# A two-layer Hymba trunk on one core: the forget gates' chain moved forward, low parts moved to GpSimd, and two plain feed-forward blocks per layer in place of three

## Chip, cores and metric

The kernel runs on one core of a Trainium2 chip. The metric is the device time of one execution in microseconds (us). Of the kernel before there are three runs: median 1271.29 us, 1268.26 to 1271.49.

Engines: PE is TensorE (matrix products; PEld is its weight load), DVE is VectorE, ACT is ScalarE, POOL is GpSimd, and SP issues DMAs.

## What is computed

512 tokens of width 1024, with 16 learned meta tokens ahead (528 columns), go through two layers:

```
xn   = rmsnorm(h);  proj = xn @ w_in            # fox q, k, v, forget logits; retention q, k, v, gate
logf = log_sigmoid(flog + b_fgate);  c = cumsum(logf)
fox: softmax(q_t.k_s / 8 + c[t] - c[s], s <= t) @ v          # 8 heads of 64
ret: sum_{s<=t} gamma^(t-s) (q_t.k_s) v_s, head norm, * silu(gate)   # 4 heads of 128
h    = h + concat(fox, ret) @ w_out
hn   = rmsnorm(h)
h    = h + (silu(hn @ w_gate) * (hn @ w_up)) @ w_down        # 2816 wide: 22 blocks of 128
```

After the second layer h is normalised once more and the meta tokens are dropped. Everything is float32, and has to stay close to float32 in precision.

## The kernel before

**Products.** Activations lie transposed, channels on partitions and tokens along the row, so h is eight tiles `h0` to `h7` of 128x528. A float32 product is made of three in the format fp32r: every operand is split into a high part (a cast) and a low part (the rest), and high x high, high x low and low x high are summed in PSUM. For weights, `convert` (L177) does this tile by tile: a 128x1024 tile `raw` comes by DMA, ScalarE casts it to `whi` (L199), and VectorE or GpSimd subtracts to make `wlo` (L202). The argument `pool` of `dense_steps` (L207) chooses: VectorE takes two subtractions of 128x512, GpSimd eight of 128x128. Activations are split into `xh` (ScalarE, L327) and `xl` (VectorE, L328).

**Norms.** A product does not wait for its norm. TensorE multiplies the raw h with its gain; the scale R of each token (`col_rstd`, L290 to L309) comes later and is multiplied in when a result leaves PSUM. `squares` (L336) makes the sum of squares `ss`, L298 adds over partitions on TensorE, L303 to L308 make R from it.

**Order.** TensorE runs in the order in which the program lists its steps: lists of small functions, into which `merge`, `spread` and `ret_places` put the steps of attention and retention at given places. The other engines' orders are chosen by a scheduler from dependencies and priorities; `tc.high_priority()` moves instructions ahead, `pin` keeps them in the program's order. PSUM has two pools: `psd` with two buffers, and `psa` with four. A product can begin only when an accumulator of its pool has been read out.

**Head of layer 0.** `start` (L1270 on) fills the time until the first data with nine matmuls on the memset tile `wide` (L1277), loads h and the first weights, and then q and k of the first pair of heads are multiplied (L225). `forget_gates` (L375) makes the eight forget logits z; `forget_sums` (L399) multiplies them by R (L403), takes log-sigmoid (Abs, Exp, Ln on ScalarE, L404 to L406; `min` and subtraction on VectorE, L407 and L408), sums along the tokens with a scan (L409) and splits the sums into `fs` (L411, L412). `q_done` (L439) reads q out of PSUM into `tq` (L442) and splits it into `qo` and `qs`; `k_done` (L453) does so for k into `kc` and `kx`, and puts the sums of the head into rows of `kc` (L467, its "own" rows). The scores (L519) multiply kc and kx with qo and qs, so the sums c[t] - c[s] come out of the same product. `ropes` (L1254) makes the rotation tables `cr` and `sr`, scaled by R.

**Feed-forward stage.** The first three of 22 blocks are plain: gate and up as full products over eight tiles of x (L225). In layer 0 these are 96 matmuls of 264 columns per block, in layer 1, which needs only the 512 real tokens, 48 of 512. `g_done` (L840, L843) reads the gate, `u_done` (L851, L852) the up part. The other 19 blocks are `Unit`s: gate and up together as a two by two block product with seven products in place of eight, 84 matmuls of half the columns each (L907). A Unit needs combined activations, the tiles `th` and `tl`, which `x_forms` (L860 on) makes from h through the tile `S` (L868 to L872, split at L151), and combined weights (L941, L942, L948, L954, split at L895 and L896). `x_forms` has four parts, put every nine steps into the plain blocks. The last tiles ahead of this stage are those of w_out's second round, whose result is added to h (L810); `scale_split` then makes xh and xl of the stage.

**Tail.** The last layer ends with the final norm, whose squares are added by VectorE (L1138) and then over the partitions on TensorE (`sums`).

Of the kernel before, what the change touches and what calls it, by code (L numbers as in the profile page):

```python
# [10 lines left out]
F32 = mybir.dt.float32  # L11
# [10 lines left out]
FH = 8  # L22
# [5 lines left out]
PLAIN = 3  # L28
# [11 lines left out]
def hybrid_kernel(ctx, tc, x_t, w_in, w_fl, w_out, w_gate, w_up, w_down, vecs, b_fg, rope, decay, mask, ident, out_t):  # L40
# [14 lines left out]
    nc.vector.memset(msk[:, 0:T - 128], 0.0)  # L55
# [11 lines left out]
    nc.vector.memset(onec, 1.0)  # L67

# [330 lines left out]
    def forget_sums(l, st):  # L399
# [7 lines left out]
        nc.vector.tensor_scalar(z, z, bfg[:, l:l + 1], 0.0, ALU.add, ALU.min)  # L407
        nc.vector.tensor_sub(z, z2, z)  # L408
# [24 lines left out]
    def fox_dense(l, g, ly, real, st):  # L433
# [20 lines left out]
        def k_done(ps):  # L454
# [3 lines left out]
            for s in range(2):  # L458
# [8 lines left out]
                (nc.gpsimd if g else nc.vector).tensor_scalar(kc[b0:b0 + 32 + FH, :], f_tiles[0].bitcast(F32), pick[:, hd:hd + 1], 0.0, ALU.mult, ALU.add)  # L467
# [345 lines left out]
    def out_proj(l, rnd, mix, real):  # L813
# [4 lines left out]
                                rnd == 0 or m2 < 2, rnd == 1 and m2 == 1) for m2 in range(NK // 2)], [])  # L818

    def ffn(l, st, real, last):  # L820
# [235 lines left out]
        for r, (f0, f1) in enumerate(ROUNDS):  # L1056
            for f in range(f0, f1):
                if f < PLAIN:
                    steps += dense_steps(w_gate[l, f], [(0, xs, NK, QC, g_done(f) if f else held.append)], banks=f == 1)
                    steps += dense_steps(w_up[l, f], [(0, xs, NK, QC, u_done(f))])  # L1060
                    continue
# [28 lines left out]
        else:  # L1090
# [34 lines left out]
            def square_b(m):  # L1125
                if m == 0:
                    t = fft("S", F32, (128, 6, w), 2)
                    fin["one"] = [t[:, i, 0:nb] for i in range(3)]
                    fin["acc"], fin["rb"], fin["tb"] = (t[:, i, 0:nb] for i in range(3, 6))
                    d = fin["acc"]  # L1130
                elif m < NK - 3:
                    fin["sq", m] = d = tt("sq")[:, 0:nb]
                else:
                    d = fin["one"][m - NK + 3]
# [101 lines left out]
        for i in range(HB):  # L1236
            steps.insert(NK + 4 + 9 * i, x_forms(i))
# [8 lines left out]
    def layer(l):  # L1246
# [68 lines left out]
        if l == 0:  # L1315
            plan += [lambda: squares(ly, FULL, True, False)] + qk[:-2] + [first_parts] + gates + qk[-2:] + stats + [lambda: ly["wait"].pop(0)()] + sums + [lambda: ly["wait"].pop(0)()]
# [9 lines left out]
        for g in range(2):  # L1326
            main, rest = fs[g]
            m0, r0, places = (((7 if l else 10.5, 31 if l else 32.5), (34, 40.5), (13, 33.5, 35.5, 37.5, 39, 40.5, 43, 44, 47.5, 48)),
# [12 lines left out]
                      ret_places(2, 26, 23.5, 24.5, 32, 28, 33.5, 36, 56.5, 40.5, 57.5),  # L1341
# [82 lines left out]
```

## Time and profile before

| | |
|---|---|
| median of three runs | 1271.29 us |
| lowest, highest run | 1268.26, 1271.49 us |
| profiled execution | 1268.53 us |
| its span, first to last instruction | 1266.7 us |
| TensorE busy | 1251.2 us, 99% |
| VectorE busy | 991.9 us, 78% |
| ScalarE busy | 704.8 us, 56% |
| GpSimd busy | 273.3 us, 22% |
| DMA | 116.19 MB, 92 GB/s mean |

A row of the timeline gives the start and the duration in us, the engine, the line, the operation, out<-in by the program's names with their shape, how many instructions the row groups, and in brackets how long the engine sat idle ahead of it and what ended that. Durations of neighbours on an engine overlap a little (matmuls more than others), so the time that an instruction takes away from its engine is the distance of two starts. A row of windows gives, for a stretch, the busy time of each engine with its instructions, the granted clock of TensorE as a share of full speed, the DMA share and GB/s. Numbers behind a name (`kc_105`) tell instances of a tile apart.

### The profile page before, as it was taken

To read this page: it belongs to the slowest core of one execution; us is meant where nothing else is said; L and a number is where in the kernel's file an instruction comes from. 1 tells how busy PE (TensorE), PEld (TensorE's weight loads), DVE (VectorE), ACT (ScalarE), POOL (GpSimd) and SP (SyncE) were. 2 spreads that over 40 slices of the span, in tenths; PEclk is the share of its full clock that TensorE was granted. 3 is DMA by queue.
4 is the path that set the end of the run, shared out by engine and by line. 5 is a ranking of instruction groups with operands and counts; after the bars stand their busy time and mean duration, and the time that the engine had idled before them with its cause. 6 is when DMAs were issued, how large, how long until landed. Compare 5 with 4: busy or idle time off the path is not lost.

```text
span 1266.7 us, 23526 instructions
## 1 busy us (share of the span) xinstructions
PE 1251.2 (99%) x9225; PEld 1194.1 (94%) x9225; DVE 991.9 (78%) x1804; ACT 704.8 (56%) x1301; POOL 273.3 (22%) x539
## 2 busy tenths in 40 slices
PE   9999999999999999999999999999999999999997
PEld 8899999999999999999999989998789999999996
DVE  8887756779988888887786877567899888888867
ACT  6766655676444444444466766557764444444445
POOL 3455546420000000000126556554100000000000
PEclk9999999999999999999999999999999999999999
DMA  6122222223333333332322122222223333333321
GB/s 218 50 76 75 76 77 72 72 67 118 104 97 100 100 101 100 101 101 84 101 77 84 60 86 74 70 90 67 100 94 123 100 101 101 100 101 101 100 84 67
DMA packets 43342, 116.19 MB, mean 92 GB/s; under 512 B 5088, under 2 KB 12000, under 8 KB 43232
## 3 DMA queue, kind: packets, MB, share of 16 engines
q1 hardware_dynamic: 42800, 114.41, 28.1%
q8 instruction: 72, 1.18, 0.4%
q14 instruction: 38, 0.31, 0.1%
q10 hardware_dynamic: 432, 0.29, 0.1%
HBM read 112.58 MB, written 2.10 MB: 91 GB/s over the span
## 4 chain that ended last, share of the span: by engine, by line
PE 93%; ACT 3%; DVE 3%; issue 1%; DMA 0%; ACTq 0%; DVEq 0%
PE psd L225 30%; PE psa L907 18%; PE psd L1042 14%; PE psd L907 13%; PE psa L225 5%; PE psa L1042 4%; PE psa L429 2%; PE psa L519 2%; PE psa L589 1%; PE psa L756 1%; PE psa L722 1%; ACT whi L199 1%; PE psa L298 0%; ACT xh L327 0%; DMA raw<-w_in 0%
## 5 line engine op out<-in xcount | busy, mean ns | idle before, releaser
L202 POOL TENSOR_TENSOR wlo<-raw,whi 128x128 fp32r<-128x128 f32 x504 | 258.2, 548 | 260.1 <-ACT whi L199 259.7
L225 PE MATMUL psd<-xh,whi 128*128 128x264 f32 (+1 forms) x792 | 195.5, 314 | 0.2 <-DVE tq L442 0.2
L225 PE MATMUL psd<-xl,whi 128*128 128x264 f32 (+1 forms) x792 | 186.7, 303 | 0.6 <-DVE xl L328 0.6
L225 PE MATMUL psd<-xh,wlo 128*128 128x264 f32 (+1 forms) x792 | 187.0, 304 | 0.0
L225 PEld LDWEIGHTS psd<-xh,whi 128*128 128x128 f32 x792 | 128.6, 189 | 5.0 <-issue 0.6
L225 PEld LDWEIGHTS psd<-xh,wlo 128*128 128x128 f32 x792 | 127.2, 188 | 6.2 <-DVE wlo L202 0.4
L225 PEld LDWEIGHTS psd<-xl,whi 128*128 128x128 f32 x792 | 127.8, 189 | 5.4 <-DVE xl L328 1.4
L199 ACT CAST whi<-raw 128x512 fp32r<-128x512 f32 (+1 forms) x168 | 97.9, 613 | 41.5 <-PE psd L225 28.4
L895 ACT CAST whi<-raw 128x1024 fp32r<-128x1024 f32 (+2 forms) x62 | 54.9, 885 | 51.3 <-PE psd L907 39.8
L895 ACT CAST fwhi<-raw 128x1024 fp32r<-128x1024 f32 (+2 forms) x62 | 55.6, 897 | 47.5 <-PE psd L907 40.0
L122 POOL MEMSET kc<- 64x528 f32 x2 | 1.1, 533 | 345.4 <-PE psa L907 345.4
L896 DVE TENSOR_TENSOR wlo<-raw,whi 128x1024 fp32r<-128x1024 f32 (+2 forms) x62 | 62.9, 1014 | 12.7 <-ACT whi L895 12.6
L896 DVE TENSOR_TENSOR fwlo<-raw,fwhi 128x1024 fp32r<-128x1024 f32 (+2 forms) x62 | 64.0, 1032 | 11.1 <-ACT fwhi L895 10.9
L907 PE MATMUL psa<-th,whi 128*128 128x264 f32 (+1 forms) x232 | 65.4, 282 | 0.0
L907 PE MATMUL psa<-th,wlo 128*128 128x264 f32 (+1 forms) x232 | 65.4, 282 | 0.0
L907 PE MATMUL psa<-tl,whi 128*128 128x264 f32 (+1 forms) x232 | 65.3, 282 | 0.0
L907 PE MATMUL psa<-th,fwhi 128*128 128x264 f32 (+1 forms) x224 | 63.4, 283 | 0.0
L907 PE MATMUL psa<-tl,fwhi 128*128 128x264 f32 (+1 forms) x224 | 63.3, 283 | 0.0
L907 PE MATMUL psa<-th,fwlo 128*128 128x264 f32 (+1 forms) x224 | 63.2, 282 | 0.0
L536 ACT ACTIVATE pr<-pr,nmax 128x144 f32<-128x144 f32 (+1 forms) x64 | 36.8, 576 | 45.4 <-DVE nmax L523 26.1
L895 ACT CAST fwhi<-S 128x1024 fp32r<-128x1024 f32 x20 | 21.0, 1049 | 68.6 <-PE psa L907 66.5
L973 ACT COPY e<-psa 128x264 f32<-128x264 f32 (+1 forms) x114 | 42.8, 376 | 28.4 <-PE psa L907 24.1
(365 smaller groups left out, 4041.2 us busy)
## 6 DMA issues: line engine op xcount, KB each, us to landing
raw<-w_in SPq DMA_DIRECT2D x54, 512.0 KB, 3.5
raw<-w_gate SPq DMA_DIRECT2D x44, 512.0 KB, 3.9
fraw<-w_up SPq DMA_DIRECT2D x38, 512.0 KB, 3.5
raw<-w_down SPq DMA_DIRECT2D x64, 256.0 KB, 2.9
raw<-w_out SPq DMA_DIRECT2D x16, 512.0 KB, 3.4
raw<-w_down SPq DMA_DIRECT2D x32, 192.0 KB, 2.5
raw<-w_up SPq DMA_DIRECT2D x6, 512.0 KB, 3.5
h<-x_t SPq DMA_DIRECT2D x8, 264.0 KB, 4.5
```

What stands on the lines that cost most here:

```text
L199: pin(nc.scalar.copy(hi, job["raw"][:, c0:c1]), pinned)
L202: pin(sub(lo[:, c:c + step], job["raw"][:, c0 + c:c0 + c + step], hi[:, c:c + step].bitcast(F32)), pinned)
L225: nc.tensor.matmul(ps[1][b][:, 0:c1 - c0], w[:, wk, :], x[:, c0:c1], start=(k == 0 and i == 0), stop=(k == n - 1 and i == 2))
L429: nc.tensor.transpose(ps[:, 128 * j:128 * j + 128], src[:, o:o + 128], idt)
L519: nc.tensor.matmul(sc[0:nq, 0:c1 - c0], qq[:, q0:q0 + nq], kk[:, c0:c1], start=(i == 0), stop=(i == 1))
L536: nc.scalar.activation(pr, pr, AF.Exp, bias=nmax[0:nq], scale=-1.0, accum_out=rsum)
L589: nc.tensor.matmul(po[:, c0:SEQ], v[:, j, :], pp[:, j, META + c0:T], start=(j == 0 and i == 0), stop=(j == 4))
L895: nc.scalar.copy(hi, src)
L896: nc.vector.tensor_sub(lo, src, hi.bitcast(F32))
L907: nc.tensor.matmul(bank()[:, 0:b.shape[-1]], a[:, o + k, :], b, start=(fresh and k == 0 and i == 0), stop=(k == n - 1 and i == 2), skip_gr ...
L973: nc.scalar.copy(self.t["e"][:, i], self.t["x"][:, 0:w])
L1042: nc.tensor.matmul(v[:, 0:c1 - c0], a[:, s * n + k, :], b[:, c0:c1], start=(k == 0 and i == 0), stop=(k == n - 1 and i == 2))
```

## The change

It has five parts.

1. `PLAIN` goes from 3 to 2: the third block of each layer becomes a Unit, and `x_forms` is put every seven steps.
2. The low parts of the plain blocks' weights, four tiles per layer, and of the last two tiles of w_out's second round go from VectorE to GpSimd.
3. In layer 0, `forget_sums` stands ahead of `q_done` and `k_done` and is given priority as a whole; the subtraction ahead of the scan is taken into the scan (add, then subtract). Of the two copies of the sums into `kc`, one is made by VectorE with priority and one by ScalarE.
4. The memset of `msk` goes from VectorE to GpSimd, and some places of steps are shifted.
5. In the tail, one more pair of squares is added on VectorE, and TensorE's sum has three operands in place of four.

```diff
-PLAIN = 3
+PLAIN = 2
...
-    nc.vector.memset(msk[:, 0:T - 128], 0.0)
...
+    nc.gpsimd.memset(msk[:, 0:T - 128], 0.0)
...
-        nc.vector.tensor_scalar(z, z, bfg[:, l:l + 1], 0.0, ALU.add, ALU.min)
-        nc.vector.tensor_sub(z, z2, z)
-        nc.vector.tensor_tensor_scan(z2, z, z, 0.0, ALU.add, ALU.max)
-        with ExitStack() if l else tc.high_priority():
+            nc.vector.tensor_scalar(z, z, bfg[:, l:l + 1], 0.0, ALU.add, ALU.min)
+            nc.vector.tensor_tensor_scan(z2, z2, z, 0.0, ALU.add, ALU.subtract)
             nc.scalar.copy(f_tiles[0][0:FH], z2)
...
-                (nc.gpsimd if g else nc.vector).tensor_scalar(kc[b0:b0 + 32 + FH, :], f_tiles[0].bitcast(F32), pick[:, hd:hd + 1], 0.0, ALU.mult, ALU.add)
+                own, of = kc[b0:b0 + 32 + FH, :], f_tiles[0].bitcast(F32)
+                if g:
+                    nc.gpsimd.tensor_scalar(own, of, pick[:, hd:hd + 1], 0.0, ALU.mult, ALU.add)
+                elif s:
+                    nc.scalar.activation(own, of, AF.Copy, scale=pick[:, hd:hd + 1])
+                else:
+                    with tc.high_priority():
+                        nc.vector.tensor_scalar(own, of, pick[:, hd:hd + 1], 0.0, ALU.mult, ALU.add)
...
-                                rnd == 0 or m2 < 2, rnd == 1 and m2 == 1) for m2 in range(NK // 2)], [])
+                                True, rnd == 1 and m2 == 1) for m2 in range(NK // 2)], [])
...
-                    steps += dense_steps(w_gate[l, f], [(0, xs, NK, QC, g_done(f) if f else held.append)], banks=f == 1)
-                    steps += dense_steps(w_up[l, f], [(0, xs, NK, QC, u_done(f))])
+                    steps += dense_steps(w_gate[l, f], [(0, xs, NK, QC, g_done(f) if f else held.append)], True, banks=f == 1)
+                    steps += dense_steps(w_up[l, f], [(0, xs, NK, QC, u_done(f))], True)
...
+                sum_b(5)
                 v = psum_a()[:, 0:nb]
-                sums(v, [fin["one"][0], fin["acc"]] + fin["one"][1:])
+                sums(v, [fin["one"][0], fin["acc"], fin["one"][1]])
...
-            steps.insert(NK + 4 + 9 * i, x_forms(i))
+            steps.insert(NK + 4 + 7 * i, x_forms(i))
...
-            plan += [lambda: squares(ly, FULL, True, False)] + qk[:-2] + [first_parts] + gates + qk[-2:] + stats + [lambda: ly["wait"].pop(0)()] + sums + [lambda: ly["wait"].pop(0)()]
+            plan += [lambda: squares(ly, FULL, True, False)] + qk[:-2] + [first_parts] + gates + qk[-2:] + stats + sums + [lambda: ly["wait"].pop(0)()] * 2
```

**VectorE at the head of layer 0.** From R (L308) on, this is its order before:

```order
L308 SCALAR_TENSOR_TENSOR R<-nwt,R 128x528
L442 SCALAR_TENSOR_TENSOR tq<-psd,R 128x528
L403 SCALAR_TENSOR_TENSOR z<-z,R 8x528
L1258 SCALAR_TENSOR_TENSOR cr<-cr,R 128x528
L450 TENSOR_TENSOR qs_427<-tq,qo_103 64x528
L456 SCALAR_TENSOR_TENSOR tq<-psd,R 128x528
L450 TENSOR_TENSOR qs_431<-tq,qo_104 64x528
L407 TENSOR_SCALAR z<-z,bfg 8x528
L473 SCALAR_TENSOR_TENSOR pd_115<-psa,R 128x264 x2
L408 TENSOR_TENSOR z<-z_435,z 8x528
L465 TENSOR_TENSOR kx_447<-tq,kc_105 64x528
L409 SCALAR_TENSOR_TENSOR z_435<-z 8x528
```

In the changed kernel the same place reads (the lines are those of the changed file: L440 is q's tq, L454 k's, L408 the scan, L478 the pd of values, L410 the low part of fs):

```order
L308 SCALAR_TENSOR_TENSOR R<-nwt,R 128x528
L403 SCALAR_TENSOR_TENSOR z<-z,R 8x528
L1264 SCALAR_TENSOR_TENSOR cr<-cr,R 128x528
L440 SCALAR_TENSOR_TENSOR tq<-psd,R 128x528
L407 TENSOR_SCALAR z<-z,bfg 8x528
L454 SCALAR_TENSOR_TENSOR tq<-psd,R 128x528
L448 TENSOR_TENSOR qs_436<-tq,qo_103 64x528
L408 SCALAR_TENSOR_TENSOR z_425<-z_425,z 8x528
L478 SCALAR_TENSOR_TENSOR pd_115<-psa,R 128x264
L448 TENSOR_TENSOR qs_440<-tq,qo_104 64x528
L478 SCALAR_TENSOR_TENSOR pd_115<-psa,R 128x264
L410 TENSOR_TENSOR fs<-z_425,fs 8x528
```

Z and cr now stand ahead of q's tq, and the scan ahead of the second half of q. What follows up to the two copies into kc was, before,

```order
L465 TENSOR_TENSOR kx_452<-tq,kc_106 64x528
L1258 SCALAR_TENSOR_TENSOR sr<-sr,R 128x528
L412 TENSOR_TENSOR fs<-z_435,fs 8x528
L644 SCALAR_TENSOR_TENSOR pd_116<-psd,R 128x528
L467 TENSOR_SCALAR kc_105<-fs,pick 40x528
L467 TENSOR_SCALAR kc_106<-fs,pick 40x528
```

and is now

```order
L463 TENSOR_TENSOR kx_446<-tq,kc_105 64x528
L472 TENSOR_SCALAR kc_105<-fs,pick 40x528
L463 TENSOR_TENSOR kx_451<-tq,kc_106 64x528
L1264 SCALAR_TENSOR_TENSOR sr<-sr,R 128x528
L649 SCALAR_TENSOR_TENSOR pd_116<-psd,R 128x528
```

The first copy (L472) moved ahead of the second kx, sr and the pd of the retention's values; the second copy left VectorE.

**VectorE at the head of the feed-forward stage, layer 0.** From the last xl to the reading of the first gate block sg, before (the S tiles are those of `x_forms`; wlo are low parts of plain blocks; L869 to L872 make S, L151 splits):

```order
L869 TENSOR_TENSOR S_4359<-S_4359 128x264
L871 SCALAR_TENSOR_TENSOR S_4359<-h5_78,vec_85,S_4359 128x264 x2
L872 SCALAR_TENSOR_TENSOR S_4359<-h5_78,vec_85,S_4359 128x264
L151 TENSOR_TENSOR tl0_4283<-S_4286,th0_4282 128x1056
L305 TENSOR_TENSOR nwt_4271<-R_4270 128x528
L151 TENSOR_TENSOR tl0_4283<-S_4359,th0_4282 128x1056
L307 SCALAR_TENSOR_TENSOR nwt_4271<-psa_4264,nwt_4271 128x264
L307 SCALAR_TENSOR_TENSOR nwt_4271<-psa_4265,nwt_4271 128x264
L202 TENSOR_TENSOR wlo_4344<-raw_4341,whi_4343 128x512
L308 SCALAR_TENSOR_TENSOR R_4270<-nwt_4271,R_4270 128x528
L202 TENSOR_TENSOR wlo_4344<-raw_4341,whi_4343 128x512
L843 SCALAR_TENSOR_TENSOR sg_4279<-psd_4149,R_4270 128x528
```

and in the changed kernel (L874 to L877 make S there, L848 reads sg):

```order
L151 TENSOR_TENSOR tl0_4309<-S_4379,th0_4308 128x1056
L877 SCALAR_TENSOR_TENSOR S_4432<-h6_79,vec_84,S_4432 128x264
L305 TENSOR_TENSOR nwt_4297<-R_4296 128x528
L874 TENSOR_TENSOR S_4485<-S_4485 128x264
L307 SCALAR_TENSOR_TENSOR nwt_4297<-psa_4290,nwt_4297 128x264
L307 SCALAR_TENSOR_TENSOR nwt_4297<-psa_4291,nwt_4297 128x264
L151 TENSOR_TENSOR tl1_4311<-S_4432,th1_4310 128x1056
L308 SCALAR_TENSOR_TENSOR R_4296<-nwt_4297,R_4296 128x528
L876 SCALAR_TENSOR_TENSOR S_4485<-h7_80,vec_84,S_4485 128x264
L848 SCALAR_TENSOR_TENSOR sg_4305<-psd_4166,R_4296 128x528
```

The low parts are gone from here, and the forms of the third and the fourth pair of tiles (S_4432, S_4485, and tl1) stand ahead of sg, which they did not before. In full the stretch has, before, six L202, eight operations on S and two tl; now one sum of squares, twelve operations on S and three tl (two in layer 1).

**GpSimd at the end of layer 0's attention.** Before, its last low part is that of the second tile of w_out's second round, and memsets for layer 1 follow:

```order
L202 TENSOR_TENSOR wlo_3600<-raw_3597,whi_3599 128x128 x8
L202 TENSOR_TENSOR wlo_3758<-raw_3755,whi_3757 128x128 x8
L202 TENSOR_TENSOR wlo_3879<-raw_3876,whi_3878 128x128 x8
L122 MEMSET kc0_8390 64x528
L91 MEMSET qo0_8388 64x528
```

In the changed kernel six more tiles follow:

```order
L202 TENSOR_TENSOR wlo_3878<-raw_3875,whi_3877 128x128 x8
L202 TENSOR_TENSOR wlo_3931<-raw_3928,whi_3930 128x128 x8
L202 TENSOR_TENSOR wlo_4014<-raw_4011,whi_4013 128x128 x8
L202 TENSOR_TENSOR wlo_4080<-raw_4077,whi_4079 128x128 x8
L202 TENSOR_TENSOR wlo_4182<-raw_4179,whi_4181 128x128 x8
L202 TENSOR_TENSOR wlo_4272<-raw_4269,whi_4271 128x128 x8
L202 TENSOR_TENSOR wlo_4373<-raw_4370,whi_4372 128x128 x8
L122 MEMSET kc0_8429 64x528
```

Of these, wlo_3931 and wlo_4014 are the last two tiles of w_out, and the other four gate and up of the two plain blocks. GpSimd does 48 subtractions more per layer.

More of the change, by code (lines that the diff above doesn't have):

```diff
@@ L1327, in layer @@
             main, rest = fs[g]
[L1328 removed]
+            m0, r0, places = (((7 if l else 11, 31 if l else 32.5), (34, 40.5), (13, 33.5, 35.5, 38, 39, 40.5, 43, 44, 47.5, 48)),
                               ((0.5, 31.5), (32, 40), (13, 33.5, 35.5, 39.5, 39, 41.5, 43, 44, 47.5, 48)))[g]
```

10 lines of the change are left out of this document (5 added, 5 removed).

## The prediction

> **What bounds the kernel now.** I read the busy line of the page first, then the waits of TensorE (PE), then single stretches of the timeline.
>
> ```profile
> PE 1251.2 (99%) x9225; PEld 1194.1 (94%) x9225; DVE 991.9 (78%) x1804; ACT 704.8 (56%) x1301; POOL 273.3 (22%) x539
> ```
>
> TensorE is busy for 1251.2 of 1266.7 us, so time can come from three places only: fewer matmul columns, the idle 15 us, and stretches in which TensorE runs at a lower clock. The waits of TensorE, largest first (releaser, total, times, longest):
>
> ```profile
> PE psa L519 <- DVE kc L467: 3.1, 1, 3.1
> PE psa L1277 <- DVE wide L63: 2.0, 1, 2.0
> PE psa L519 <- DVE mixt L593: 0.7, 1, 0.7
> PE psa L756 <- DVE rsl L151: 0.7, 2, 0.4
> PE psd L225 <- DVE xl L328: 0.6, 2, 0.4
> PE psd L225 <- DVE tq L442: 0.2, 1, 0.2
> PE psa L1164 <- ACT S L1135: 0.2, 1, 0.2
> ```
>
> The longest stands at the head of layer 0: the first score (L519) waits for kc, which takes the sums of the forget gates. The timeline of TensorE there, and the window behind it (the column after the busy times is the granted clock):
>
> ```profile
> 29.34 0.48 PE L225 MATMUL psd<-xh,whi 128*128 128x264 f32 x2 [0.25 <-DVE tq L442]
> ...
> 37.14 0.40 PE L225 MATMUL psd<-xh,wlo 128*128 128x264 f32 x2
> 40.60 0.17 PE L519 MATMUL psa<-kc,qo 128*16 128x16 f32 x1 [3.06 <-DVE kc L467]
> ```
>
> ```profile
> 41.00:46.00 5.00, 5.00 (x32) 5.00 (x31) 2.66 (x13) 1.97 (x8) 1.21 (x3) 0.66 0.30 105
> ```
>
> The place costs twice: 3.06 us of waiting, and then 5 us at a mean clock of 0.66, which is 0.34 x 5 = 1.7 us of lost work.
>
> **The change part by part: the forget gates.** VectorE (DVE) at this head, start and duration:
>
> ```profile
> 28.49 0.71 DVE L442 SCALAR_TENSOR_TENSOR tq<-psd,R 128x528 f32<-128x528 f32 x1
> 29.11 0.98 DVE L403 SCALAR_TENSOR_TENSOR z<-z,R 8x528 f32<-8x528 f32 x1
> 30.03 0.69 DVE L1258 SCALAR_TENSOR_TENSOR cr<-cr,R 128x528 f32<-128x528 f32 x1
> 30.75 0.86 DVE L450 TENSOR_TENSOR qs<-tq,qo 64x528 fp32r<-64x528 f32 x1
> ...
> 34.20 0.69 DVE L408 TENSOR_TENSOR z<-z,z 8x528 f32<-8x528 f32 x1
> ...
> 36.71 0.70 DVE L465 TENSOR_TENSOR kx<-tq,kc 64x528 fp32r<-64x528 f32 x1
> 37.45 0.71 DVE L1258 SCALAR_TENSOR_TENSOR sr<-sr,R 128x528 f32<-128x528 f32 x1
> ...
> 39.06 0.71 DVE L644 SCALAR_TENSOR_TENSOR pd<-psd,R 128x528 f32<-128x528 f32 x1
> 39.80 1.26 DVE L467 TENSOR_SCALAR kc<-fs,pick 40x528 fp32r<-40x528 f32 x2
> ```
>
> In the new order z and cr stand ahead of q's tq, so tq starts at 28.49 + (30.75 - 29.11) = 30.13 instead of 28.49: 1.64 us late. Tq frees the two-buffer accumulator psd for which the matmul at 29.34 waits, so that wait grows from 0.25 to about 1.9 us, and the score is asked for at 37.14 + 0.40 + 1.64 = 39.2. By 30.75 VectorE has done the same set in both orders. From there the old order needs until 39.80 + 1.26 = 41.06 for both kc, which is 10.3 us. The new order leaves out, ahead of the first kc, the subtraction L408 (0.69), the second kx (0.70), sr (0.71), the pd of L644 (0.71) and the second kc (half of 1.26), 3.4 us together: kc is there at about 37.6, ahead of 39.2. ScalarE makes the second kc in place of VectorE; it reads the same sums and is asked for later. So the score starts at 39.2 in place of 40.60: **-1.4 us**. The longest wait is then 1.9 us and no longer 3.06. No wait of that length in mid-stream is in this trace; its bounds are the 0.7 us waits, after which no slow stretch is seen, and the 3.06 us wait with its 1.7 us. 1.9 lies about midway (1.88); I take the side of the 0.7, because the 2.0 us that TensorE waits for wide are the only other wait of that length, and the window of that place shows a full clock: **-1.7 us**, with 0 kept for the range. ```profile
> 0.00:10.00 10.00, 7.73 (x34) 6.53 (x35) 8.00 (x26) 6.23 (x11) 1.44 (x9) 1.00 0.82 277
> ```
>
> The Trainium skill, page "TensorE: Matmul & The Clock Gate" (Part 1: The HAM clock gate), has the clock halve after an idle window of about 3.4 us that runs freely; this trace saw it after 3.06 us already, so the figure does not hold strictly here.
>
> **One more block of seven products.** A plain block of feed-forward columns is 96 matmuls of 264 columns in layer 0 and 48 of 512 in layer 1; a Unit is 84 of 264 or 256.
>
> ```profile
> 322.50 0.28 PE L907 MATMUL psa<-xh,whi 128*128 128x264 f32 x1
> ...
> 323.95 0.28 PE L907 MATMUL psd<-xh,whi 128*128 128x264 f32 x1
> ```
>
> ```profile
> 927.98 0.39 PE L225 MATMUL psa<-xh,wlo 128*128 128x512 f32 x1
> 928.21 0.42 PE L225 MATMUL psd<-xh,whi 128*128 128x512 f32 x1
> ```
>
> Twelve matmuls of 264 take 323.95 - 322.50 = 1.45 us, 0.121 each: layer 0 saves 12 x 0.121 = 1.45. In layer 1 one of 512 takes 0.23: 48 x 0.23 = 11.0, against 84 x 0.121 x 256/264 = 9.9, so 1.1 us. Together **-2.6 us**, certain in so far as the operands come in time.
>
> **Low parts on GpSimd (POOL).** This is where the change can lose. The head of the feed-forward stage of layer 0 has no reserve on VectorE: it is busy for 54.51 of 55 us. The first block's gate value there (sg), its surroundings, and the same in layer 1:
>
> ```profile
> 275.00:330.00 55.00, 55.00 (x456) 54.85 (x455) 54.51 (x91) 36.94 (x59) 0.00 (x0) 1.00 0.35 115
> ```
>
> ```profile
> 296.64 0.42 DVE L869 TENSOR_TENSOR S<-S 128x264 f32<-128x264 f32 x1
> ...
> 298.35 1.26 DVE L151 TENSOR_TENSOR tl<-S,th 128x1056 fp32r<-128x1056 f32 x1
> ...
> 302.00 0.68 DVE L202 TENSOR_TENSOR wlo<-raw,whi 128x512 fp32r<-128x512 f32 x1
> 302.60 0.70 DVE L308 SCALAR_TENSOR_TENSOR R<-nwt,R 128x528 f32<-128x528 f32 x1
> ...
> 303.82 0.70 DVE L843 SCALAR_TENSOR_TENSOR sg<-psd,R 128x528 f32<-128x528 f32 x1
> ```
>
> ```profile
> 305.14 0.40 PE L225 MATMUL psd<-xh,whi 128*128 128x264 f32 x2
> ```
>
> ```profile
> 927.33 0.68 DVE L843 SCALAR_TENSOR_TENSOR sg<-psd,R 128x512 f32<-128x512 f32 x1
> ```
>
> Sg (L843) frees the accumulator that the matmul at 305.14 takes: it ends at 304.5, so 0.6 us are left; in layer 1 it ends at 928.01 and the matmul starts at 928.21, 0.2 us. Between the last xl and sg the new order takes out six halves of low parts, 0.60 us each (302.60 - 302.00), 3.6 us. It puts in, since the first Unit comes one block earlier, one sum of squares (0.70), four S forms (0.42 each or less) and in layer 0 one tl (1.26): 3.6 us in layer 0, 2.4 in layer 1. So VectorE has as much to do there as before in layer 0, and 1.2 us less in layer 1. What is new is GpSimd beside it: two tiles, 16 subtractions, in that stretch. What the two engines do to each other stands elsewhere in the trace:
>
> ```profile
> 252.71 3.89 POOL L202 TENSOR_TENSOR wlo<-raw,whi 128x128 fp32r<-128x128 f32 x8 [2.99 <-ACT whi L199]
> ```
>
> ```profile
> 715.15 5.43 POOL L202 TENSOR_TENSOR wlo<-raw,whi 128x128 fp32r<-128x128 f32 x8 [3.01 <-ACT whi L199]
> ...
> 717.58 0.96 DVE L465 TENSOR_TENSOR kx<-tq,kc 64x528 fp32r<-64x528 f32 x1
> ...
> 718.47 0.94 DVE L305 TENSOR_TENSOR nwt<-r 128x512 f32<-128x512 f32 x1
> ```
>
> Eight subtractions take 3.89 us alone and 5.43 beside VectorE, and VectorE's operations with two operands in SBUF grow from about 0.69 to 0.95. In that stretch of 5.4 us some four such operations met GpSimd, so a tile costs VectorE about 4 x 0.26 = 1.0 us; the other ones read PSUM and were not longer. The bounds per tile are 0 (GpSimd falls into gaps) and 8 x 0.26 = 2.1 us (each subtraction meets one). I take 1.0, the measured tile. Two tiles give 2.0 us: layer 0 waits 2.0 - 0.6 = 1.4 us at the second up block, layer 1 2.0 - 1.2 - 0.2 = 0.6. The last two tiles fall beside the low part of the first Unit, which the first product waits for: another 1.0 in each layer. Ahead of the last xl, three tiles cost 3.0 us where six halves (3.6 us) went away: 0, with up to 1 us either way, as these xl are already waited for (0.6 us above). With t us per tile the sum is 2 x (2t + t) - 0.6 - 1.4 = 6t - 2.0: **+4.0 us** at t = 1.0, bounds 0 and 6 x 2.1 - 2.0 = +10.6, and up to 2.7 more ahead of the last xl (three tiles of 2.1 against 3.6). GpSimd's own pace holds: 5.43 us a tile against 48 matmuls of 0.121 us, 5.8. The next loads wait for GpSimd's last subtraction instead of VectorE's; with three buffers of raw a tile has the time of two tiles to land, so I cost the loads at nothing, and if that cover is gone they are part of the 10.6.
>
> The rule that speaks against the change is in the Trainium skill, page "SBUF — State Buffer" (SBUF: two separate sides): a VectorE operation with two SBUF inputs and a GpSimd operation exclude each other for a whole instruction. By it every subtraction would cost VectorE all of its own time; the rows above show 0.26 us, about half of that, so here it holds in kind and less in size.
>
> **The small edits.** The memset of msk leaves VectorE, where it stood ahead of wide:
>
> ```profile
> 0.89 0.39 DVE L55 MEMSET msk<- 128x400 f32 x1 [0.89 <-PEq L1412]
> ...
> 2.02 4.21 PE L1277 MATMUL psa<-wide,ones 128*128 128x512 f32 x9 [2.02 <-DVE wide L63]
> ```
>
> The nine warm-up matmuls then start 0.39 us earlier, and the first product follows them at 6.03 to 6.23: **-0.3 us**, bounds 0 (the first weights are late instead) and -0.4. The tail drops one matmul of 240 columns and adds one VectorE sum ahead of it; the shifted places of the retention steps move work of VectorE past a wait of 0.7 us: both between -0.7 and +0.7, taken as 0.
>
> **Sum.** -1.4 - 1.7 - 2.6 + 4.0 - 0.3 = -2.0 us. The profiled execution took 1268.53 us (span 1266.7 and 1.83 around it), which gives 1266.5. The median of the runs shown is 1271.29, 2.8 us above that execution, so on its scale the same change would read 1269.3; I name 1266.5, and let the range hold both.
>
> **Rivals.**
>
> *GpSimd fits into gaps.* VectorE's operations on PSUM and its waits for ScalarE give GpSimd its turns, and the 4.0 us fall away: 1268.5 - 6.0 = 1262.5. For it: GpSimd is idle in both heads, and starts on a tile as soon as its cast is there, up to two blocks ahead. Against it: 54.51 of 55 us leave no gaps in layer 0.
>
> *The two engines alternate strictly.* Each subtraction meets a two-operand operation of VectorE, 0.26 us each. Place: the stretch between the last xl and sg in each layer; price +10.6 in place of +4.0, so 1262.5 + 10.6 = 1273.1, 1275.8 with the 2.7 ahead of xl, and a slow stretch of 1.7 us more behind any single wait over 3 us. The change is slower than before from the point where the heads cost the 6.0 us that the other parts give: 6t - 2.0 = 6.0, t = 1.33 us per tile, a third more than the tile that I measured. For it: nearly all of VectorE's work there has two SBUF operands.
>
> *The wait at the head changes its place only.* Q's tq comes late by 1.64 us, or by more if z waits for R; if 1.9 us of idle time lower the clock as 3.06 did, or kc waits for ScalarE's chain of Abs, Exp and Ln, the 1.7 us stay: 1266.5 + 1.7 = 1268.2, and up to 1269.6 if the score does not start earlier either. That is also the case in which the first part does not do what it says.
>
> **How the numbers follow.** The forecast (1263 to 1270) has 0.40, the gaps 0.28, the alternation 0.22, the moved wait 0.10. About 0.3%, 3.8 us, is what a measurement of this kernel can tell from no change. Faster by more: all of the gaps and a quarter of the forecast, 0.38. Slower by more: most of the alternation, 0.18. The rest, 0.44, is within. The range goes from 1260.0, the low bounds together, to 1274.0, which leaves the upper half of the alternation out. The forecast's own range is 1263 to 1270.
>
> **What would show it.** Right at the head: the first score within 1.5 us of 39.2, no wait for kc, a clock of 1.00 from 39 to 46, and a wait of about 1.9 us for tq. Right on the blocks: 12 matmuls fewer in layer 0, and layer 1's third block taking 9.9 us instead of 11.0. Right on GpSimd: waits of TensorE for sg and the first Unit's low part of 0.3 to 1.5 us each, VectorE operations of 0.85 to 1.0 us beside GpSimd in the heads. Wrong: waits for sg above 3 us, or none, or a lowered clock after the tq wait. What I may miss is a wait in a stretch that I take as unchanged, above all the retention steps after 40 us.

## The result, and the profile after

The change makes the kernel slower: 1287.69 us (median of 4 runs, 1286.31 to 1288.93) against 1270.37 (1268.26 to 1271.49), ratio 1.0138 with a 95% interval of 1.012 to 1.0156, which is 17 us. The prediction was 1266.5 us, with a range up to 1274.0. The profiled execution spans 1285.8 us. Its busy line:

```profile
PE 1255.5 (98%) x9247; PEld 1196.8 (93%) x9247; DVE 1001.6 (78%) x1790; ACT 713.6 (56%) x1311; POOL 336.4 (26%) x636
```

TensorE is idle for 30.3 us instead of 15.5. The waits of TensorE in the changed kernel, by what ended them (its lines: L848 is sg, L912 the Units, L1047 the down products, L594 the attention's product with v, L727 the retention scores):

```profile
PE psd L225 <- DVE sg L848: 5.1, 2, 2.8
PE psd L1047 <- ACT ah L150: 2.4, 1, 2.4
PE psa L912 <- ACT e L978: 1.9, 1, 1.9
PE psa L594 <- DVE ptl L151: 1.8, 3, 0.8
PE psd L225 <- DVE tq L440: 1.8, 1, 1.8
PE psd L225 <- ACT mxh L150: 1.6, 2, 1.0
...
PE psa L1169 <- ACT S L1140: 0.9, 1, 0.9
```

The wait for kc is gone, and a number of others have come in its place. First the head of layer 0, from the timeline of TensorE and the windows:

```profile
30.41 0.48 PE L225 MATMUL psd<-xh,whi 128*128 128x264 f32 x2 [1.75 <-DVE tq L440]
...
38.44 0.17 PE L524 MATMUL psa<-kc,qo 128*16 128x16 f32 x1
```

```profile
41.00:46.00 5.00, 5.00 (x43) 5.00 (x42) 4.51 (x16) 4.26 (x14) 1.64 (x5) 1.00 0.36 105
```

The score stands at 38.44 in place of 40.60, with a full clock behind it. Then the heads of the two feed-forward stages, where most of the time went:

```profile
309.83 0.77 PE L225 MATMUL psd<-xh,whi 128*128 128x264 f32 x2 [2.85 <-DVE sg L848]
...
337.04 0.51 PE L1047 MATMUL psa<-ah,fwhi 128*128 128x264 f32 x2 [0.39 <-ACT ah L150]
338.46 0.51 PE L1047 MATMUL psa<-al,fwhi 128*128 128x264 f32 x2 [0.92 <-DVE al L151]
...
939.62 0.47 PE L225 MATMUL psd<-xh,whi 128*128 128x512 f32 x1 [2.26 <-DVE sg L848]
...
950.15 0.39 PE L912 MATMUL psa<-th,fwhi 128*128 128x256 f32 x1 [1.91 <-ACT e L978]
...
969.91 0.50 PE L1047 MATMUL psd<-ah,fwhi 128*128 128x512 f32 x1 [2.44 <-ACT ah L150]
971.19 0.50 PE L1047 MATMUL psd<-al,fwhi 128*128 128x512 f32 x1 [0.78 <-DVE al L151]
```

```profile
310.00:315.00 5.00, 5.00 (x30) 5.00 (x31) 5.00 (x9) 3.14 (x5) 1.23 (x3) 0.67 0.26 79
...
950.00:955.00 5.00, 4.85 (x28) 4.85 (x29) 4.96 (x8) 2.56 (x5) 0.00 (x0) 0.66 0.35 105
```

In both layers TensorE waits for sg and at the first down product. It also runs three stretches of 3.4 us at half clock, which cost 1.7 us each: in layer 0 one behind the wait for sg (a mean of 0.67 over the 5 us from 310), in layer 1 one behind the wait for e (0.66 from 950) and one behind the first down product (0.72 from 971 to 977). VectorE is busy for 9.81 of the 10 us ahead of the first of them. Its timeline ahead of sg in layer 0:

```profile
302.15 1.52 DVE L151 TENSOR_TENSOR tl<-S,th 128x1056 fp32r<-128x1056 f32 x1
303.59 0.69 DVE L877 SCALAR_TENSOR_TENSOR S<-h,vec,S 128x264 f32<-128x264 f32 x1
304.20 0.96 DVE L305 TENSOR_TENSOR nwt<-R 128x528 f32<-128x528 f32 x1
...
307.51 0.95 DVE L308 SCALAR_TENSOR_TENSOR R<-nwt,R 128x528 f32<-128x528 f32 x1
308.38 0.68 DVE L876 SCALAR_TENSOR_TENSOR S<-h,vec,S 128x264 f32<-128x264 f32 x1
308.99 0.69 DVE L848 SCALAR_TENSOR_TENSOR sg<-psd,R 128x528 f32<-128x528 f32 x1
```

Tl takes 1.52 us where it took 1.26, R 0.95 where it took 0.70, the short S forms 0.68 where they took 0.48; sg, which reads one operand from PSUM, is not longer. Sg begins at 308.99, when it began at 303.82 before.

Where the 19 us of span came from can be read by comparing the same steps in both traces (the times are those of the kernel before). At the product with v at 61 us the changed kernel is 4.0 us ahead; at 76 us, behind the first retention head, 0.6 us; at the end of layer 0's attention (262.8) it is level; when the first norm of layer 1 is summed (649.6) it is 7.7 us behind; at the retention scores at 868.6 in layer 1 it is 7.4 behind, when the second norm of layer 1 is summed (919.5) 8.9, and at the end 19.1. So nearly all of it is lost in the two feed-forward stages, the second with the tail.

### The profile page after: what moved, and what is told of

Same layout as the page of the kernel before. It is cut to its first block, busy times and chain, and to the rows that moved or that the text cites. A ratio compares the mean times of both kernels' runs of the same rounds, so it can differ in the third digit from the quotient of the medians.

```text
span 1285.8 us, 23691 instructions
## 1 busy us (share of the span) xinstructions
PE 1255.5 (98%) x9247; PEld 1196.8 (93%) x9247; DVE 1001.6 (78%) x1790; ACT 713.6 (56%) x1311; POOL 336.4 (26%) x636
## 4 chain that ended last, share of the span: by engine, by line
PE 83%; DVE 10%; ACT 5%; issue 1%; DMA 1%; DVEq 0%; ACTq 0%; SPq 0%
PE psd L225 22%; PE psa L912 19%; PE psd L1047 14%; PE psd L912 13%; PE psa L1047 4%; PE psa L225 3%; PE psa L427 2%; PE psa L594 1%; PE psa L524 1%; PE psa L761 1%; PE psa L727 1%; ACT whi L199 1%; DVE ss L348 1%; ACT xh L327 1%; DVE tl L151 1%
## 5 line engine op out<-in xcount | busy, mean ns | idle before, releaser
L202 POOL TENSOR_TENSOR wlo<-raw,whi 128x128 fp32r<-128x128 f32 x600 | 321.3, 571 | 273.2 <-ACT whi L199 252.7
L225 PE MATMUL psd<-xh,whi 128*128 128x264 f32 (+1 forms) x744 | 183.4, 315 | 7.5 <-DVE sg L848 5.1
L225 PE MATMUL psd<-xh,wlo 128*128 128x264 f32 (+1 forms) x744 | 174.2, 303 | 0.0
L225 PE MATMUL psd<-xl,whi 128*128 128x264 f32 (+1 forms) x744 | 173.9, 302 | 0.0
L225 PEld LDWEIGHTS psd<-xh,whi 128*128 128x128 f32 x744 | 121.1, 190 | 12.1 <-issue 6.4
L225 PEld LDWEIGHTS psd<-xh,wlo 128*128 128x128 f32 x744 | 119.3, 189 | 5.1
L225 PEld LDWEIGHTS psd<-xl,whi 128*128 128x128 f32 x744 | 120.1, 189 | 3.4 <-DVE xl L328 0.2
L912 PE MATMUL psa<-th,wlo 128*128 128x264 f32 (+1 forms) x248 | 70.5, 284 | 0.0
L912 PE MATMUL psa<-th,whi 128*128 128x264 f32 (+1 forms) x248 | 70.4, 284 | 0.0
L912 PE MATMUL psa<-tl,whi 128*128 128x264 f32 (+1 forms) x248 | 70.2, 283 | 0.0
L912 PE MATMUL psa<-th,fwhi 128*128 128x264 f32 (+1 forms) x232 | 65.9, 284 | 1.9 <-ACT e L978 1.9
L912 PE MATMUL psa<-th,fwlo 128*128 128x264 f32 (+1 forms) x232 | 65.8, 283 | 0.0
L912 PE MATMUL psa<-tl,fwhi 128*128 128x264 f32 (+1 forms) x232 | 65.8, 283 | 0.0
```

The source lines that it names most:

```text
L202: pin(sub(lo[:, c:c + step], job["raw"][:, c0 + c:c0 + c + step], hi[:, c:c + step].bitcast(F32)), pinned)
L225: nc.tensor.matmul(ps[1][b][:, 0:c1 - c0], w[:, wk, :], x[:, c0:c1], start=(k == 0 and i == 0), stop=(k == n - 1 and i == 2))
L912: nc.tensor.matmul(bank()[:, 0:b.shape[-1]], a[:, o + k, :], b, start=(fresh and k == 0 and i == 0), stop=(k == n - 1 and i == 2), skip_gr ...
```

## The experiments

All ratios are against the kernel before, run on the same chip. I call **P** the theory of the ports: GpSimd beside VectorE slows it. **R** is the theory of the reserve: with one plain block less ahead of it, the first Unit comes before VectorE can have its operands ready, whoever makes the low parts.

### One part undone, one part alone

The first run undoes part 2 in the changed kernel:

```diff
-[(0, xs, NK, QC, u_done(f))], True)
+[(0, xs, NK, QC, u_done(f))])
```

(the same for gate and for w_out).

> The changed kernel with part 2 undone: the low parts of the plain blocks and of w_out's last tiles are VectorE's again; two plain blocks, the gates' order and the small edits stay. Theory P (ports: each GpSimd subtraction makes a two-operand operation of VectorE 0.26 us longer) says that the waits for sg (2.9 and 2.3 us) and the slow stretches behind them go: 8 to 14 us less than the changed kernel, near 1275. Theory R (reserve: with one block less ahead of the first Unit, VectorE's work for it has too little time, whoever makes the low parts) says that VectorE now has 0.6 us per half tile more to do and the waits stay: 1285 to 1292.

Measured: 1286.75 us, ratio 1.0131 (1.0114 to 1.0148), no better than the changed kernel. The waits for sg are gone, and others take their place:

```profile
320.68 0.39 PE L912 MATMUL psa<-th,fwhi 128*128 128x264 f32 x1 [3.85 <-ACT fwhi L900]
...
952.72 0.39 PE L912 MATMUL psa<-th,fwhi 128*128 128x256 f32 x1 [4.27 <-ACT fwhi L900]
```

So P alone does not explain the result. The opposite run has part 2 alone on the kernel before (three plain blocks, 64 subtractions per layer on GpSimd):

> The kernel before with part 2 alone: three plain blocks, six tiles with them and two of w_out per layer on GpSimd. P: VectorE is slowed in the same way, 8 to 16 us more than the kernel before. R: no loss, since the first Unit is as late as before, 1267 to 1271.

Measured: 1285.34 us, ratio 1.0119 (1.0103 to 1.0134). P holds as well, and R's forecast for this run does not. The waits of TensorE, largest first:

```profile
PE psd L225 <- DVE sg L843: 5.1, 2, 2.9
PE psa L519 <- DVE kc L467: 3.1, 1, 3.1
PE psd L225 <- ACT whi L199: 2.8, 1, 2.8
```

The third of these is not a slower VectorE. It stands at 326.90, at the third plain block, and comes from a late load: GpSimd's last subtraction on a tile ends at 322.55, the load into its buffer is issued at 322.58, ScalarE waits 4.54 us for it, and the cast that TensorE needs comes next in ScalarE's order. A stretch at half clock follows (1.7 us). So part 2 has two costs here, and the prediction had put the loads at nothing. In the changed kernel, with its two plain blocks, this wait does not occur.

Part 1 alone is `PLAIN = 2` and `7 * i` on the kernel before:

> The kernel before with part 1 alone: two plain blocks, x_forms every seven steps, low parts on VectorE. P: the 2.6 us of saved matmuls show, 1266 to 1269. R: 6 to 12 us more than the kernel before, with waits of TensorE at the second up block and the first Unit.

Measured: 1284.74 us, ratio 1.0117 (1.0102 to 1.0132). R holds, with more loss than its 6 to 12 us: the waits at the first Unit are those of the run without part 2.

```profile
PE psa L907 <- ACT fwhi L895: 8.1, 2, 4.3
PE psa L519 <- DVE kc L467: 3.1, 1, 3.1
...
PE psd L1042 <- DVE al L151: 0.9, 1, 0.9
PE psa L1042 <- DVE al L151: 0.9, 1, 0.9
```

The window from 312 to 318 us, the sum that VectorE makes for the first Unit, and TensorE's wait for its cast:

```profile
312.00:318.00 6.00, 2.63 (x22) 2.42 (x21) 6.00 (x11) 2.61 (x4) 0.00 (x0) 1.00 0.00 0
```

```profile
316.66 0.69 DVE L942 TENSOR_TENSOR S<-S,raw 128x512 f32<-128x512 f32 x1
318.48 0.39 PE L907 MATMUL psa<-th,fwhi 128*128 128x264 f32 x1 [3.85 <-ACT fwhi L895]
```

VectorE is busy for all 6 us, while TensorE has work for 2.63. The place of the second plain block's wait differs from what was expected: not sg, but the first Unit's second product (fwhi, the cast of a sum that VectorE makes) and the first down product. Each of the two parts loses some 15 us alone, and together they lose 16 (the changed kernel, 1287.69, against the run further below that has only its other parts, 1272.05). I read this as both exhausting the same reserve of VectorE, so that undoing one does not help.

The profiled executions show what these us are: idle time of TensorE, half clock, and the 2.6 us of saved matmuls on the other side. With part 1 alone the span is 14.6 us longer than before (1281.3 against 1266.7). TensorE is idle for 11.2 us more (26.7 against 15.5), and half clock costs 6.8 us more (8.5 against 1.7): 5.1 behind the waits of the first Unit (319 to 323 and 947 to 955), and 1.7 at the head of layer 0, which part 1 does not touch. Less 2.6, that is 15.4. The changed kernel has a span 15.7 us longer than the run with only its other parts (1285.8 against 1270.1): 11.8 us more of idle time (30.3 against 18.5) and 5.1 of half clock, less 2.6, are 14.3. So about a third of the loss is the lower clock behind waits.

Part 3 alone, the gates:

> The kernel before with part 3 alone: the forget sums first, the fused scan, the own rows of kc on VectorE and ScalarE. If the forecast's step holds: the first score near 38.5, full clock, 3 us less, 1267. If the gain is given back in the first retention head, as the trace of the changed kernel suggests (4.0 us ahead of the kernel before at 61, 0.6 ahead at 76): 0 to 1 us less.

Measured: 1267.09 us, ratio 0.9976 (0.9966 to 0.9985), 3 us less. The score stands at 38.41, the clock is full. In the two profiled executions the run is 3.7 us ahead at 45 us, and 1.4 us at the end (spans of 1265.3 against 1266.7). New waits stand in the first retention head:

```profile
65.58 0.45 PE L727 MATMUL psa<-rqh,rkh 128*128 128x400 f32 x1 [0.51 <-DVE ptl L151]
67.30 0.55 PE L427 MATMUL psa<-idt,pr 128*128 128x128 f32 x3 [0.18 <-DVE sd L732]
68.77 0.51 PE L761 MATMUL psa<-rsh,rvh 128*128 128x512 f32 x1 [0.20 <-ACT rsh L150]
69.52 0.50 PE L761 MATMUL psa<-rsl,rvh 128*128 128x512 f32 x1 [0.24 <-DVE rsl L151]
```

So part of the gain is given back at these waits, which TensorE now reaches some 3 us earlier. The forecast step holds in the main.

### What GpSimd costs VectorE

Here GpSimd works for nothing beside the kernel before:

```diff
+                if job.get("dum"):
+                    for d in range(c, c + step):
+                        nc.gpsimd.tensor_sub(dum, job["raw"][:, c0 + d], hi[:, d].bitcast(F32))
```

> The kernel before, unchanged in what VectorE and TensorE do, and beside it GpSimd subtracts the same 64 pieces of 128x128 per layer as in the run with part 2 alone (raw minus whi) into a scratch tile that nobody reads. No operand waits for GpSimd, but buffers of raw and whi come free only behind it. P (ports): VectorE's operations beside it grow from 0.69 to 0.95 us, some 0.26 us per piece, with no relief from low parts: over 15 us more than the kernel before. If part 2 lost time because low parts came late from GpSimd, and not because VectorE is slowed: within 3 us of the kernel before.

Measured: 1291.47 us, ratio 1.0165 (1.0144 to 1.0185), 21 us more. VectorE's low parts take 0.93 us in place of 0.68. In this run no operand comes from GpSimd, so the time is lost to the slowing of VectorE and to buffers that come free later; the run does not separate these two. The same with one operand in SBUF, `nc.gpsimd.tensor_scalar(dum, job["raw"][:, c0 + d], 1.0, 0.0, ALU.mult, ALU.add)`:

> As the scratch subtraction, but with one operand in SBUF (raw times 1 plus 0). P in the wording of any GpSimd operation that reads SBUF: a loss in proportion to GpSimd's busy time, over 8 us. If it takes two read operands on GpSimd to slow VectorE: within 3 us of the kernel before.

Measured in one execution 1276.05 us (span 1274.2, some 7 us over the kernel before); another took 7015.69 us, for which no trace stands and which I leave unexplained. The low parts and the sums of squares on VectorE (L203, L352), by groups between 285 and 312 us (line, operation, count, busy, mean ns), first of the run with the subtraction, then of this one:

```profile
L203 DVE TENSOR_TENSOR wlo<-raw,whi 128x512 fp32r<-128x512 f32 x7 | 6.3, 926 | 0.0
L352 DVE TENSOR_TENSOR ss<-ss,sq 128x528 f32<-128x528 f32 x6 | 5.6, 937 | 0.0
```

```profile
L203 DVE TENSOR_TENSOR wlo<-raw,whi 128x512 fp32r<-128x512 f32 x8 | 5.8, 748 | 0.0
L352 DVE TENSOR_TENSOR ss<-ss,sq 128x528 f32<-128x528 f32 x6 | 4.5, 757 | 0.0
```

With two operands on GpSimd an operation of VectorE grows by about 0.24 us, with one by 0.06. The 7 us, of one execution, lie between the two forecasts: under the 8 of any reading of SBUF and over the 3 of the other. GpSimd holds the raw tiles in both runs (it is busy for 338.8 us here and 362.7 with the subtraction, 273.3 before), so late raw buffers do not explain most of the 21 us. Late buffers of whi, which only the subtraction reads, were not tested apart.

GpSimd for the two w_out tiles only (`rnd == 0 or m2 < 2` becomes `True`):

> The kernel before with only the last two tiles of w_out's second round on GpSimd, 16 subtractions per layer, at about 272 to 285 in layer 0, just ahead of the feed-forward blocks. P at a strict 0.26 us per piece: 4.2 us of VectorE time against 2.4 saved, 1.8 us late per layer at the xl that are already waited for: 2 to 5 us more than the kernel before. If VectorE still has room there: within 1 us.

Measured: 1268.49 us, ratio 0.9987 (0.9978 to 0.9996): no loss, rather a gain of 1 to 2 us. There VectorE has room. Not all of the gain comes from these tiles: the profiled execution is 2.3 us shorter (1264.4 against 1266.7), of which 1.7 are the stretch at half clock at the head of layer 0, which this execution lacks.

### What the block costs, and VectorE's reserve

Four plain blocks in place of three:

> The kernel before with four plain blocks in place of three. R: the kernel before has just enough time ahead of the first Unit, so a fourth block frees nothing and costs its matmuls, 1.45 us in layer 0 and 1.1 in layer 1: 2 to 3 us more than the kernel before. If VectorE's reserve also sets waits behind the first Unit: no more than 1 us.

Measured: 1274.53 us, ratio 1.0031 (1.002 to 1.0042), 3.9 us more; 2.6 was worked out, and one new wait of 1.5 us at a down product is in the trace, 4.1 together. So the size of the saving per block fits, though no run shows it by itself. Two plain blocks, and six additions of the sum of squares left out:

```diff
+                    if att or k == NK - 1:
                         nc.vector.tensor_add(acc[:, c], acc[:, c], sq[:, c])
```

> Two plain blocks with VectorE's low parts (part 1 alone), and six of the seven additions of the sum of squares ahead of the feed-forward stage left out in both layers, some 3.7 us of VectorE per layer; the second norm's sum lacks six of its eight parts. R (VectorE's time ahead of the first Unit is what is missing): the waits for fwhi, 3.9 and 4.3 us, shrink by about 3.7 us each and the slow stretches behind them go: 8 to 13 us less than with part 1 alone, 1272 to 1277. If the first Unit waits for something that VectorE's load does not set (loads of the weights, ScalarE's casts): no change, near 1285.

Measured: 1278.54 us, ratio 1.0062 (1.0047 to 1.0078), 6 us less than with part 1 alone, short of the 8 to 13 forecast. Less work on VectorE takes the wait for fwhi from 3.85 and 4.26 us to nothing in layer 0 and 0.69 in layer 1; waits of 0.8 us for the low part, fwlo, stay. That is R. But at the first down product stand longer waits, where there were 0.9 us, and half clock behind them (3.4 and 1.7 us lost):

```profile
335.77 0.51 PE L1043 MATMUL psa<-ah,fwhi 128*128 128x264 f32 x2 [2.31 <-ACT ah L150]
337.06 0.81 PE L1043 MATMUL psa<-al,fwhi 128*128 128x264 f32 x2 [0.78 <-DVE al L151]
...
963.71 0.49 PE L1043 MATMUL psd<-ah,fwhi 128*128 128x512 f32 x1 [1.65 <-ACT ah L150]
964.87 0.80 PE L1043 MATMUL psd<-al,fwhi 128*128 128x512 f32 x1 [0.66 <-DVE al L151]
```

The control, the kernel before with the same additions left out:

> The kernel before with the same six additions per layer left out, as the control. R: nothing waits for VectorE there now, so 0 to 1 us less. Should it become more than 2 us faster, the run with two plain blocks and fewer additions cannot be read as relief of the first Unit alone.

Measured: 1269.18 us, ratio 0.9995 (0.9986 to 1.0004): with three blocks, taking out the same work gains next to nothing. The second limit is the first down product. Its round ends with block 2, which was plain and is now a Unit, whose activation is ready only after VectorE and ScalarE have worked on its last product. The rounds cut at 2, 6, 10, 14 and 18 separate the two:

```diff
-ROUNDS = ((0, 3), (3, 7), (7, 11), (11, 15), (15, 19), (19, 22))
+ROUNDS = ((0, 2), (2, 6), (6, 10), (10, 14), (14, 18), (18, 22))
```

> Part 1 alone, with the down products' rounds cut at 2, 6, 10, 14 and 18 blocks in place of 3, 7, 11, 15 and 19, so that the first down product takes the two plain blocks only and not the first Unit's result. R with a second place (the first down product waits for the first Unit's activations): the 0.9 us waits at the down product go, the waits for fwhi of 3.9 and 4.3 us stay: 2 to 4 us less than part 1 alone, 1281 to 1283. If the down product's place is only a follower of the first wait: no change, 1285.

Measured: 1292.74 us, ratio 1.0171 (1.0156 to 1.0187), 8 us more and not less: a miss. The waits at the first down product are gone, those for fwhi are as they were, and new ones of 2.1 and 3.1 us stand at the end of both stages, the second with 3.4 us lost to half clock behind it. With less work on VectorE as well:

> As above, and six of seven additions of the sum of squares ahead of the feed-forward stage left out in both layers (the second norm's sum lacks six of its eight parts). R: with the first Unit's wait relieved by 3.7 us of VectorE time and the down product's by the cut of the rounds, both places are clear and the 2.6 us of saved matmuls show at last: 1266 to 1271. If a third limit stands behind them, over 1273.

Measured: 1279.42 us, ratio 1.0067 (1.0054 to 1.0081), and not the 1266 to 1271 of R. In the heads 0.8 us of waiting are left in layer 0 and 1.4 in layer 1. The long waits are at the ends:

```profile
628.08 0.51 PE L1043 MATMUL psd<-ah,whi 128*128 128x264 f32 x2 [2.08 <-ACT ah L150]
...
1242.21 0.60 PE L908 MATMUL psa<-ah,whi 128*128 128x272 f32 x1 [3.11 <-ACT ah L150]
```

So a third limit came with this cut. The last round had three Units for four pairs of down tiles, and the pair left over stood between the last Unit and the products that need its result. Now it has four Units, and this cover is gone. The saved matmuls of part 1 never showed as a shorter time in any run.

### The small edits

The changed kernel with `PLAIN = 3`, `9 * i` and part 2 undone:

> The changed kernel without parts 1 and 2: the gates' order, the memset, the shifted places and the tail stay, on three plain blocks with VectorE's low parts. Parts 3 to 5 alone: the run with part 3 alone was 2.6 us under the kernel before, the memset gives 0.3 to 0.4 at the start: 3 us less, 1266 to 1267. If the shifted places cost what their wait for ptl and sd suggests (the changed kernel loses 3.4 us between 61 and 76): no gain over part 3 alone, 1267 to 1269.

Measured: 1272.05 us, ratio 1.002 (1.0011 to 1.003), 2.5 us more than the kernel before, in place of 3 less. With the old places put back:

```diff
-(7 if l else 11, ... 38, 39, ... 36, 56.5, 49, 57.5) ... 60.6, 64.1, 63.6, 64.2
+(7 if l else 10.5, ... 37.5, 39, ... 36, 56.5, 40.5, 57.5) ... 60, 64.1, 63, 64.2
```

> The changed kernel without parts 1 and 2 and with the places of the kernel before: the gates' order, the memset and the tail are left. If the shifted places cost what lies between the run with part 3 alone (2.6 us under the kernel before) and the run with parts 3 to 5 (2.4 us over it): 3 us under the kernel before, 1266 to 1267. If the tail or the memset cost it: near the kernel before or above.

Measured: 1269.17 us, ratio 0.9993 (0.9984 to 1.0002). So the shifted places cost 2.9 us, in a wait for mxh and mxl at the last tiles of w_out (0.62 and 0.23 us in layer 0, 1.02 and 0.22 in layer 1), which is not there with the old places, and some in the first retention head. What still lies between this run and part 3 alone, 2 us, is by elimination the tail or the memset. The trace shows the tail's wait at 0.9 us in place of 0.2. The memset lets the warm-up matmuls start at 1.59 in place of 2.02, but in this run that lead is gone at the first product (5.96 against 5.99). The two were not run apart.

The two parts that gained, the gates and the two w_out tiles, together:

> The kernel before with part 3 (the gates' order) and the last two w_out tiles of each layer on GpSimd. The first alone gave 2.6 us, the second 1.6 us with an interval that ends near 0.5; the places do not touch: 3 to 4 us under the kernel before, 1266 to 1267. If both gains are only executions without a lowered clock at the head of layer 0: no more than the first alone.

Measured: 1266.40 us (1266.18 to 1266.91), ratio 0.9965 (0.9953 to 0.9978), 4.4 us under the kernel before and 21 under the changed one.

## Why the prediction was wrong, point by point

**The gates: right.** Score at 38.44 (39.2 forecast), no wait for kc, 1.75 us of waiting for tq (1.9 forecast), full clock. Alone it gave 3 us of the 3.1. That the two agree so closely is in part luck: the head gave 3.7 in the trace, and part of it is lost again at the first retention head, which I had only named as what I may miss.

**The block: this step failed.** I booked -2.6 us for two plain blocks and called it certain "in so far as the operands come in time", and then did not check that they do. Part 1 alone costs 15 us. A plain block is cover for the first Unit: leaving it out brings the Unit's deadline forward by a block of TensorE time, 11.6 us (96 matmuls of 0.121 us), while VectorE is spared the block's low parts and its reading, some 5 us (four halves of 0.60 and four operations of 0.6 on sg, tq, their product and al), and VectorE had no idle time there. The row that says so, 54.51 of 55 us, I had quoted myself and used for GpSimd only. The run with fewer additions shows this cause: with 3.7 us of VectorE work less per layer, of the 8.1 us of waiting for fwhi 0.7 are left. Two more costs of the missing block I had not looked at: the first down product now waits for a Unit (1.8 us in part 1 alone, 5.4 once the first Unit comes early), and 5.1 us go to half clock behind the new waits.

**GpSimd: the mechanism was right, the size was off.** I took 1.0 us per tile out of bounds of 0 and 2.1. Between the last xl and sg VectorE's operations are, summed and against their durations without GpSimd, 3.55 us longer in layer 0 (17 subtractions meet them) and 3.74 in layer 1 (19): 1.6 to 1.7 us per tile. With these, my own sums give waits for sg of 3.55 - 0.6 = 2.95 and 3.74 - 1.4 = 2.3 us; measured were 2.85 and 2.26. By 6t - 2.0 the term would have been 7.6 to 8.2 us in place of 4.0. The tile from which I took 1.0 stood in a stretch where VectorE also read PSUM; in the feed-forward head nearly all its operations read two operands in SBUF. I had written that as an argument for the rival and yet priced by the other stretch. Over the whole stage 48 subtractions cost VectorE some 6.5 us and spare it 7.2 (twelve halves of 0.60; its busy time is 1001.6 us with both layers' subtractions on GpSimd and 1002.9 without): VectorE's total hardly changes, but sg, in the middle of it, comes late. The point from which the change loses, 1.33 us per tile, was passed. Part 2 alone costs 15 us, which also holds the late load of 2.8 us and 5.1 us of half clock behind the waits; neither was in the term. The Trainium skill, page "SBUF — State Buffer" (SBUF: two separate sides), has a VectorE operation with two SBUF inputs and a GpSimd operation that reads SBUF exclude each other for a whole instruction; that VectorE pays about 0.26 us of a subtraction of 0.46 agrees in kind, not in full.

**The lowered clock: a chance, not a term.** I let it go with the wait for kc. In the eleven profiled executions here that still have that wait of 3.0 to 3.1 us, ten show a stretch at half clock behind it (eight of 3.4 us, two of 6.8), one (the w_out tiles on GpSimd) none; of the six with 1.5 to 1.8 us of waiting for tq, one (the run without part 2) has it, five don't. So 1.7 us is about right as a mean, and a single profile cannot give it. In the feed-forward heads the new waits of the changed kernel brought three such stretches back, 5.1 us, which the sum had at nothing. I had allowed for one only in a rival, and only behind a wait over 3 us; these stand behind waits of 2.85, 1.91 and 2.44 us.

**The small edits: taken as 0, and they cost.** The shifted places cost 2.9 us by themselves, outside of the 0.7 with which I had bounded them. The 0.3 us for the memset shows in no run by itself: the first product stands at 5.60 us in the changed kernel and at 6.03 before, but at 5.96 in the run with the old places. I had not followed the places in layer 1's attention at all.

**The chance of the rival.** The rival that comes nearest to the changed kernel's trace, alternation of the two engines with slow stretches behind the waits, had 0.22 and a price that would have led to 1273 to 1277. It does not decide the result, since the run without GpSimd's part loses as much. The range was too low chiefly since no rival held the cost of the missing block: with the measured costs, the sum is -3 for the gates, +2.9 for places and some 2 for the tail or memset, and 16 for parts 1 and 2, 18 in all against 17 measured.

## What to carry to other kernels

Work on the bounding engine is also cover for the others: before taking it out, add up what the second engine must finish ahead of the new deadline, above all where it is busy for 99% of the stretch. Give a helper engine work where the main one has room, and price their contention in the stretch where it will happen, by the operands of the operations that stand there. When two parts each exhaust the same reserve, undoing one shows nothing: run each alone.

## What the runs showed of the hardware

A GpSimd subtraction with two operands in SBUF lengthens a two-operand operation of VectorE by about 0.24 us (0.68 to 0.93), one with one operand by 0.06 (0.68 to 0.75); VectorE operations that read PSUM stay as they are (h<-psd,h takes 0.69 us beside it and 0.70 without). Whether a wait of 3 us on TensorE is followed by 3.4 us at half clock (a granted clock of 0.50) differs from one execution to the next. The length of the wait does not decide it: in the changed kernel waits of 1.91 and 2.44 us were followed by such a stretch and one of 2.26 was not. In the run without part 2 a wait of 1.77 us was enough, and in the run with the scratch subtraction one of 1.29 with another of 0.54 ahead of it.
